# Seven block products for eight in four of the twelve value chunks of a two-layer encoder's first layer

## The chip, the cores and the metric

The kernel runs on one core of a Trainium2 chip. The metric is the time of one execution on the device in microseconds, median of three runs: 1988.34 us before (1987.91 to 1989.26). PE is the matrix engine, DVE the vector engine, ACT the scalar engine, POOL and SP two further engines that here mostly issue transfers.

## The reference, cut to what matters

The model is an encoder of two layers over 256 tokens of width 2048 in fp32; layer 0 mixes tokens by attention over a neighbourhood, layer 1 by grouped-query attention, and both attend to 256 memory tokens. The change touches the projection of layer 0 that makes the values `v`, 12 heads of 128:

```
def reference(x, mem, mem_norm, attn_norm, mlp_norm, a_w_in, ...):
    m = rms_norm(mem, mem_norm)
    h = x
    for i in range(DEPTH):
        n = rms_norm(h, attn_norm[i])
        if i % N_MIXERS == 0:
            z = n @ a_w_in[j]
            q, k, v, qm = jnp.split(z, [MIX_WIDTH, 2 * MIX_WIDTH, 3 * MIX_WIDTH], axis=-1)
            mix = neighbourhood_attention(split_heads(q, N_MIX_HEADS), split_heads(k, N_MIX_HEADS),
                                          split_heads(v, N_MIX_HEADS), a_rpb[j])
...
        h = h + jnp.concatenate([mix, cross], axis=-1) @ w_o[i]
        n = rms_norm(h, mlp_norm[i])
        h = h + jnp.square(jax.nn.relu(n @ w_up[i])) @ w_down[i]
    return rms_norm(h, final_norm)
```

## The kernel before

**Arithmetic.** Every fp32 operand is split into a high and a low part (`split`, L519 on ACT writes the high part, L520 on DVE the low part), and each product of two operands is three matmuls: high by high, high by low, low by high.

**Chunks and halves.** A weight chunk is 1 MB (`raw`, 128 partitions by 2048 values, a ring of three, loaded by SP). It is used in two halves of 1024 columns of storage; each half is split into one place of a ring of four `hi` and one of four `lo`. Projections of two kinds use them. "S" products (L422, `ps_s`) keep an activation's or weight's 128x128 block still and move 128x256: 24 matmuls a half. "M" products (L399, L402, L403, `ps_m`) move 128x512: 12 matmuls a half.

**Layer 0's input projection.** After the memory's keys and values and the four memory heads' queries come three groups. A group is a value projection for four heads (chunks `w_av[g*4]` to `w_av[g*4+3]`, eight halves, summed in two banks of PSUM) and then, for each of its four heads, a query chunk and a key chunk (S). When a head's key is done its attention follows: scores `sc_ps` on PE, softmax on DVE and ACT (`sc`, `nm`, `rs`), DVE's transposition `sc_t`, transfers into `pT_t` by SP, the split of `pT_t`, and `av` on PE, whose split lands in `cat`. The attention of a group's last head falls into the value projection of the next group.

**What sets the order.** `plan` lists the pieces of work and `run_all` (L456) walks through their halves in `order`. Ahead of the half that PE is to run, it issues the stages of later halves: the load 8 ahead, a `lift` 8 ahead, `pre` 5 and the split (`prep`) 3 ahead. `later(n, ...)` puts a function n halves on. A scheduler with a model of the times then sets the order of instructions on each engine; on the chip each engine runs its list in that order.

**Seven for eight, where the kernel has it already.** Layer 0's output projection uses a scheme with seven block products for eight in two chunks (`crossed_works`, L1065; PSUM `ps_x`, and `s_x`, `t_x` for sums of weight blocks). The activations' sums for it are made by `sums_ahead` (L1046): ACT copies 128x512 of `cat` into `c_x` (L1056), a transfer issued by POOL adds 256 KB to it on the way (L1057), DVE makes three sums (L1061 to L1063), and a split puts them into `a_x`. A `lift` of the same kind stands in the up-projection (L1353, L1354, `t<-b`): an ACT copy, and a transfer of 256 KB that adds.

Of the kernel before, what the change touches and what calls it, by code (L numbers as in the profile page):

```python
# [24 lines left out]
NH = 12  # L25
# [8 lines left out]
CH = 2048  # L34
HALF = CH // 2
# [11 lines left out]

CROSSED = (3, 0)
CROSSED_NB = 2
CROSSED_AT = 64  # L50

MOVING_AT = 160

# [10 lines left out]
LONGER = {"hi": 128, "lo": 128}  # L64
# [93 lines left out]
class Grain:  # L158


    def __init__(self, run, after=None, load=None, pre=None, prep=None, ahead=(8, 5, 3), lift=None):
        self.run, self.after, self.stages = run, after, (load, lift, pre, prep)
        self.ahead = ahead[0], 8, *ahead[1:]
        self.kind, self.last_block = "M", False


@with_exitstack
def encoder_kernel(ctx: ExitStack, tc: tile.TileContext, t: dict, out: bass.AP):
    nc = tc.nc
# [55 lines left out]
    for q in range(4):  # L225
        s = slice(q * 512, (q + 1) * 512)
# [151 lines left out]
    def later(n, fn, *args):  # L378
        pending.append((state["tick"] + n, fn, args))
# [48 lines left out]
    def begin():  # L428

        box["memT"] = at.cat.tile([P, KT, 512], F32R, tag="cat", name="memT")  # L430
        tiles = {}
        for w in plan[:FIRST_CHUNKS]:
            w.start(w)
        for q in range(4):
            s = slice(q % 2 * 512, q % 2 * 512 + 512)

            def memory(k):
                return split_pair(box["memT"], mem0[:, k * SEQ : (k + 1) * SEQ], G_MEM, k)

            def weights(c):  # L440
                if q % 2 == 0:
                    tiles[c] = new_half("S")
                return split(*(x[:, s] for x in tiles[c]), raws[c][:, q * 512 : (q + 1) * 512])


            for fn, n in ((memory, 4 * q), (memory, 4 * q + 1), (weights, 0), (memory, 4 * q + 2), (memory, 4 * q + 3),
                          (weights, 1), (weights, 2)):
                for ins in fn(n):
                    if q == 0:
                        pin(ins)  # L450
            for c, w in enumerate(plan[:FIRST_CHUNKS]):
# [65 lines left out]
    def split(dst_hi, dst_lo, src):  # L517

        first = nc.scalar.activation(dst_hi, src, AF.Copy)  # L519
        return first, nc.vector.tensor_tensor(dst_lo, src, dst_hi.bitcast(F32), op=ALU.subtract)  # L520
# [40 lines left out]
    def summed(ps, name, row, factor=1.0):  # L561

        s = at.work.tile([P, SEQ], F32, tag="sum_s", name=f"{name}_s")
        nc.vector.scalar_tensor_tensor(s, ps, factor, row, op0=ALU.mult, op1=ALU.mult)
        return s
# [203 lines left out]
    def values(tag, name, bufs=None):  # L769
        return at.work.tile([P, 2, NT, 512], F32R, tag=tag, bufs=bufs, name=name)  # L770

    def head_of(v, hd):
        return lambda part, kt: v[:, part, kt, hd * HD : (hd + 1) * HD]

    def put_value(dst, ps, r):
        nc.scalar.activation(dst[:, 0], ps, AF.Copy, scale=r)
        nc.vector.scalar_tensor_tensor(dst[:, 1], ps, r, dst[:, 0].bitcast(F32), op0=ALU.mult, op1=ALU.subtract)

    def put_values(v, ps, scale):
        for i in range(NT):  # L780
            put_value(v[:, :, i, :], ps[i], scale[:, i : i + 1])
# [103 lines left out]
    add_mem(1)  # L885


    GH = 4

    def a_v_done(g):  # L890
        def f(w):
            box["v", g] = values("l4", "va")
            put_values(box["v", g], w.ps, box["x_col"])
        return f

    def a_q_done(hd):
        def f(w):
# [6 lines left out]
    def a_k_done(hd):  # L904
        def f(w):
# [10 lines left out]
    def a_qm_done(hd):  # L916
        def f(w):
            if hd == 0:
                box["cat"] = at.cat.tile([P, KT, 512], F32R, tag="cat", name="cat0")
            q = at.work.tile([P, 512], F32R, tag="b_y", name="qmT")  # L920
            s = summed(w.ps, "qm", box["x_row"], SCALE)
            split(q[:, :SEQ], q[:, SEQ:], s)
            attention([(q, box["km"][:, hd, :], None, head_of(box["vm"], hd), NH + hd, box["cat"])], 1)
        return f

    for hd in range(NMH):
        add_s(t["w_aqm"][hd], get("nT"), a_qm_done(hd))
    for g in range(NH // GH):
        add_m([t["w_av"][g * 4 + c] for c in range(4)], parts_of("nT"), a_v_done(g))
        for hd in range(g * GH, (g + 1) * GH):  # L930
            add_s(t["w_aq"][hd], get("nT"), a_q_done(hd))
            add_s(t["w_ak"][hd], get("nT"), a_k_done(hd))
# [138 lines left out]
    def crossed_works(done):  # L1071
# [28 lines left out]
        def half(n, c, hf):  # L1100
# [29 lines left out]
            def run():  # L1130
# [52 lines left out]

    FIRST = ("p3", 6, 0), ("p1", 0, 1), ("p2", 2, 2)
    SECOND = ("p7", 4, 0), ("p6", 5, 1), ("p4", 1, 2), ("p5", 3, 3)

    def half_of_side(raw, hf, place=0):  # L1190
        s = slice(place // 4, place // 4 + HALF)
# [139 lines left out]
    def down_grains(layer, n, begins, ends, sooner):  # L1331
# [80 lines left out]

    def open_strassen(layer):
# [421 lines left out]
    def blocks(nb):  # L1835
        return [t["w_b"][nb * 4 + c] for c in range(4)]
# [186 lines left out]
```

## Time and profile before

| what | us |
|---|---|
| median of three runs | 1988.34 |
| the profiled execution, whole | 1987.95 |
| its span, first to last instruction | 1986.1 |
| two heads' query and key chunks ahead of the middle value group | 166.07 to 189.79 |
| middle value group | 189.79 to 212.86 |
| two heads ahead of the third value group | 235.70 to 259.43 |
| third value group | 259.43 to 282.50 |
| four heads behind it, with the `c_x` sums | 282.50 to 329.80 |

Times inside the span count from its first instruction. The 1.85 us between span and whole execution lie around the span. A row of the timeline gives the start, the duration and, in brackets, how long the engine had been idle and what released it. A group of PE rows has the modelled end of each matmul, so that the pitch from start to start says more than the duration.

### The profile page before, as it was taken

Reading aid. Unit: us, or ns where it says so; the run is one execution under the profiler, and the core shown is the slowest. Engines: PE = TensorE matmul, PEld = TensorE weight load, DVE = VectorE, ACT = ScalarE, POOL = GpSimd, SP = SyncE. Lnnn points to the kernel's source line nnn. Section 1 sums busy time; section 2 is a strip of 40 time slices with the busy share of each in tenths; the row PEclk is TensorE's granted clock in tenths of the full one; section 3 lists DMA queues with packets and bytes.
Section 4 is the critical chain, followed back from the end, with each engine's and each line's share of the span. In section 5 each row is a group of like instructions: output and inputs, shape, how many; then the busy total and the mean of one; then the engine's idle time right before and its main releaser. Section 6 shows DMA issues by size and latency. Waiting matters only on the chain.

```text
span 1986.1 us, 33222 instructions
## 1 busy us (share of the span) xinstructions
PE 1976.1 (99%) x12852; PEld 1797.4 (90%) x12852; DVE 1743.9 (88%) x2132; ACT 1450.1 (73%) x2123; POOL 156.5 (8%) x209
## 2 busy tenths in 40 slices
PE   9999999999999999999999999999999999999998
PEld 8999999899999999999998888889999999999997
DVE  7777768799999999999999869789999999999997
ACT  6655556677887778777887656668788777877786
POOL 0000000000000000000001001001000000000001
PEclk9999999999999999999999999999999999999999
DMA  8856666777777777777778765668777777777775
GB/s 296 319 195 203 207 195 195 275 223 240 228 227 236 232 226 235 232 242 227 223 227 230 266 213 176 220 207 256 238 229 227 237 224 232 236 234 240 225 225 158
DMA packets 113951, 454.57 MB, mean 229 GB/s; under 512 B 19073, under 2 KB 43777, under 8 KB 66433
## 3 DMA queue, kind: packets, MB, share of 16 engines
q1 hardware_dynamic: 92320, 414.43, 60.9%
q0 software_dynamic: 21184, 37.50, 10.7%
q8 instruction: 101, 1.65, 0.3%
q10 hardware_dynamic: 288, 0.52, 0.1%
q14 instruction: 58, 0.47, 0.1%
HBM read 397.78 MB, written 4.19 MB: 202 GB/s over the span
## 4 chain that ended last, share of the span: by engine, by line
PE 97%; DVE 1%; DMA 1%; issue 1%; ACT 0%; SPq 0%; POOL 0%; DVEq 0%; POOLq 0%; ACTq 0%
PE ps_u L422 35%; PE p L1386 10%; PE p L1389 10%; PE p L1390 10%; PE ps_s L422 9%; PE ps_m L402 7%; PE ps_m L403 7%; PE ps_m L399 7%; DMA c_x<-cat 0%; PE sc_ps L617 0%; PE sc_ps L616 0%; PE sc_ps L615 0%; PE av L711 0%; PE av L712 0%; PE av L713 0%
## 5 line engine op out<-in xcount | busy, mean ns | idle before, releaser
L422 PE MATMUL ps_u<-hT,uh 128*128 128x256 f32 x3812 | 662.9, 276 | 0.0
L422 PEld LDWEIGHTS ps_u<-hT,uh 128*128 128x128 f32 x3812 | 578.7, 188 | 4.8
L422 PE MATMUL ps_u<-hT,ul 128*128 128x256 f32 x1964 | 542.7, 276 | 0.0
L519 ACT ACTIVATE uh<-raw_U 128x1024 fp32r<-128x1024 f32 x258 | 273.4, 1061 | 157.2 <-PE ps_u L422 155.2
L422 PEld LDWEIGHTS ps_u<-hT,ul 128*128 128x128 f32 x1964 | 368.8, 188 | 0.0
L519 ACT ACTIVATE hi<-raw 128x1024 fp32r<-128x1024 f32 (+2 forms) x215 | 221.0, 1032 | 160.8 <-PE ps_m L403 81.0
L520 DVE TENSOR_TENSOR lo<-raw,hi 128x1024 fp32r<-128x1024 f32 (+2 forms) x215 | 253.3, 1184 | 85.4 <-ACT hi L519 84.6
L520 DVE TENSOR_TENSOR ul<-raw_U,uh 128x1024 fp32r<-128x1024 f32 x258 | 313.9, 1218 | 11.6 <-ACT uh L519 11.6
L520 DVE TENSOR_TENSOR tl<-t,th 128x2048 fp32r<-128x2048 f32 x120 | 274.8, 2290 | 51.7 <-ACT th L519 51.2
L519 ACT ACTIVATE th<-t 128x2048 fp32r<-128x2048 f32 x120 | 230.6, 1922 | 92.6 <-PE p L1390 92.6
L520 DVE TENSOR_TENSOR bl<-b,bh 128x1536 fp32r<-128x1536 f32 x120 | 210.1, 1751 | 0.3 <-ACT bh L519 0.3
L1354 POOL DMA_DIRECT2D t<-b x120 | 103.4, 862 | 1175.6 <-ACT t L1353 1073.8
L1386 PE MATMUL p<-th,a_s 128*128 128x512 f32 x480 | 187.4, 391 | 0.0
L1389 PE MATMUL p<-tl,a_s 128*128 128x512 f32 x480 | 187.2, 390 | 0.0
L1390 PE MATMUL p<-th,a_s 128*128 128x512 f32 x480 | 186.7, 389 | 0.0
L519 ACT ACTIVATE bh<-b 128x1536 fp32r<-128x1536 f32 x120 | 178.8, 1490 | 3.4
L422 PE MATMUL ps_s<-nT,hi 128*128 128x256 f32 x896 | 154.6, 277 | 0.0
L1389 PE MATMUL p<-bl,a_s 128*128 128x512 f32 x360 | 140.1, 389 | 0.0
L1386 PE MATMUL p<-bh,a_s 128*128 128x512 f32 x360 | 140.1, 389 | 0.0
L1390 PE MATMUL p<-bh,a_s 128*128 128x512 f32 x360 | 140.0, 389 | 0.0
L422 PEld LDWEIGHTS ps_s<-nT,hi 128*128 128x128 f32 x896 | 135.3, 188 | 0.2
L422 PE MATMUL ps_s<-nT,lo 128*128 128x256 f32 x448 | 124.2, 277 | 0.0
(343 smaller groups left out, 3713.2 us busy)
## 6 DMA issues: line engine op xcount, KB each, us to landing
raw_U<-in_w_up SPq DMA_DIRECT2D x128, 1024.0 KB, 6.3
b<-in_w_pair SPq DMA_DIRECT2D x120, 1024.0 KB, 5.8
raw<-in_w_o SPq DMA_DIRECT2D x32, 1024.0 KB, 5.0
t<-b POOLq DMA_DIRECT2D x120, 256.0 KB, 6.6
raw<-in_w_b SPq DMA_DIRECT2D x21, 1024.0 KB, 5.8
raw<-in_w_av SPq DMA_DIRECT2D x12, 1024.0 KB, 5.0
raw<-in_w_aq SPq DMA_DIRECT2D x12, 1024.0 KB, 4.9
raw<-in_w_ak SPq DMA_DIRECT2D x12, 1024.0 KB, 4.9
```

What stands on the lines that cost most here:

```text
L399: first = nc.tensor.matmul(ps, ah, hi[:, s], start=st, stop=False)
L402: nc.tensor.matmul(ps, ah, lo[:, s], start=False, stop=False)
L403: final = nc.tensor.matmul(ps, al, hi[:, s], start=False, stop=sp)
L422: ins = nc.tensor.matmul(ps, x, acts[:, k, part], start=k == n == 0, stop=k == KT - 1 and n == 2)
L519: first = nc.scalar.activation(dst_hi, src, AF.Copy)
L520: return first, nc.vector.tensor_tensor(dst_lo, src, dst_hi.bitcast(F32), op=ALU.subtract)
L1354: nc.gpsimd.dma_start(s[:, 3, :], b[:, 1, :], accum_op=ALU.add)
L1386: ins = nc.tensor.matmul(ps, a[:, 0, ai, :], hi[:, s], start=entered, stop=False, skip_group_check=True)
L1389: nc.tensor.matmul(ps, a[:, 0, ai, :], lo[:, s], start=False, stop=False, skip_group_check=True)
L1390: nc.tensor.matmul(ps, a[:, 1, ai, :], hi[:, s], start=False, stop=ends, skip_group_check=True)
```

## The change

Chunk 0 of every group, and chunk 1 of the middle group too, are computed by seven block products for eight: four of twelve chunks, eight of 24 halves. For a half, the left side is 2 x 2 blocks (two blocks of 128 rows of tokens by two blocks of 128 of the width) and the right side 2 x 2 blocks of 128x256. Seven products in three matmuls each are 21 matmuls of 128x256, in place of 12 of 128x512.

- **`combined`** makes the left sides' sums once: for each of the four pairs an ACT copy (128x512), a transfer of POOL that adds (256 KB), three DVE sums and a split. They lie in places of `cat` that heads 4 to 11 fill later. It runs from the start of the memory heads' queries on (`COMBINED_AT`).
- **The right side's sums**, per half: `lift` (an ACT copy of 512 into `s_v`, and a transfer of POOL that adds 256 KB), `pre` (two DVE sums of 128x256), `prep` (a split of 768 of the raw blocks and one of 1024 of the sums, two places of the ring and not one). `s_v` has two places, so the third crossed half's lift in a group waits until the first one's sums are split, and the fourth's until the second's.
- **`fold`** after the last crossed half of a group: two ACT copies of 512 out of `ps_x`, four DVE subtractions of 256. **`done`**: two DVE sums of 512 of `ps_m` and these, and then `put_value` from SBUF and not from PSUM.
- A value group holds four banks of PSUM and not two.
- `VALUES_ORDER` sets halves in turn: plain, crossed, plain, crossed and four plain in the first and third group (crossed halves are 6 and 7); plain, crossed, plain, crossed, plain, crossed, crossed, plain in the middle one.
- The host permutes the blocks in the crossed chunks of `w_av`. `CROSSED_AT` shifts where the output projection's crossed splits lie in the ring's place.

```
+VALUES_CROSSED = (0,), (0, 1), (0,)
+VALUES_ORDER = {1: (0, 6, 1, 7, 2, 3, 4, 5), 2: (0, 4, 1, 5, 2, 6, 7, 3)}
+COMBINED_AT = (1, 2, 6, 8)
...
+            if w.mixed:
+                order[-8:] = [order[n - 8] for n in w.mixed]
...
+    FIRST = ("p3", 6, 0), ("p1", 0, 1), ("p2", 2, 2)
+    SECOND = ("p7", 4, 0), ("p6", 5, 1), ("p4", 1, 2), ("p5", 3, 3)
...
+        def together(n):
+            k, c = pairs[n], room[:, n % 2, :4].rearrange("p (k b) j -> p k (b j)", k=2)
+            both = box["nT"][:, k : k + 2, :].bitcast(F32)
+            nc.scalar.activation(c, both[:, :, :SEQ], AF.Copy)
+            nc.gpsimd.dma_start(c, both[:, :, SEQ:], accum_op=ALU.add)
...
+        for n, at_tick in zip(range(len(pairs)), COMBINED_AT):
+            later(at_tick, together, n)
+            later(at_tick + 2, summed, n)
...
+        def fold():
+            z = room(0)
+            for n in range(NT):
+                nc.scalar.activation(z[:, 2 - 2 * n : 4 - 2 * n].rearrange("p a b -> p (a b)"), sums["two"][n], AF.Copy)
+            for d, x, y in ((3, 3, 2), (0, 3, 0), (3, 3, 1), (1, 1, 0)):
+                nc.vector.tensor_tensor(z[:, d], z[:, x], z[:, y], op=ALU.subtract)
...
+            def lift():
+                own["s"] = room(hf)
+                s, b = own["s"][:, 0:4:3], blocks()
+                nc.scalar.activation(s, b[:, 3, None, :].to_broadcast([P, 2, SEQ]), AF.Copy)
+                nc.gpsimd.dma_start(s, b[:, 0:2], accum_op=ALU.add)
+
+            def pre():
+                s, b = own["s"], blocks()
+                for d in (1, 2):
+                    nc.vector.tensor_tensor(s[:, d], s[:, d - 1], b[:, d], op=ALU.add)
+
+            def prep():
+                own["b"], own["t"] = ([at.ring.tile([P, HALF + x], F32R, tag=y, bufs=4, name=y)[:, VALUES_AT // 4 :][:, : m * SEQ]
+                                       for y, x in LONGER.items()] for m in (3, 4))
+                split(*own["b"], blocks()[:, :3].rearrange("p a b -> p (a b)"))
+                box["weights"] = split(*own["t"], own["s"].rearrange("p a b -> p (a b)"))
...
+                for products, (bh, bl) in ((FIRST, own["b"]), (SECOND, own["t"])):
+                    for name, ai, bi in products:
+                        ah, al = acts[ai]
+                        s = slice(bi * SEQ, (bi + 1) * SEQ)
...
+                            own[name] = nc.tensor.matmul(ps, ah, bh[:, s], start=st, stop=False, skip_group_check=True)
+                        nc.tensor.matmul(ps, ah, bl[:, s], start=False, stop=False, skip_group_check=True)
+                        nc.tensor.matmul(ps, al, bh[:, s], start=False, stop=sp, skip_group_check=True)
+
+            g_ = Grain(run, fold if last else None, load if hf == 0 else None, pre, prep, lift=lift)
+            g_.ahead = 7, 5, 4, 3
+            return g_
...
-        add_m([t["w_av"][g * 4 + c] for c in range(4)], parts_of("nT"), a_v_done(g))
+        crossed_values(g)
```

The order of instructions shows the change at three places. Numbers behind a name are those of the tile.

First place: DVE's list before the change, two heads ahead of the middle value group, from the split of one head's `pT_t` to the next head's query.

```order
L520 TENSOR_TENSOR lo_2036<-raw_2033,hi_2035 128x1024
L520 TENSOR_TENSOR pT_t_1820<-pT_t_1820 128x320
L599 TENSOR_TENSOR sc_1945<-sc_ps_1940,bias_1928 128x320
L601 TENSOR_TENSOR sc_1945<-sc_ps_1940,sc_1945 128x320
L573 TENSOR_REDUCE nm_1948<-sc_1945 128x2
L520 TENSOR_TENSOR lo_2067<-raw_2033,hi_2066 128x1024
L578 RECIPROCAL rs_1953<-sm_1949 128x2
L564 SCALAR_TENSOR_TENSOR q_s_2029<-ps_s_1963,x_row_970 128x256
```

The same stretch of DVE's list in the changed kernel (L528 is the `split` line there, L989 the sums of `pre`, `raw_2140` the first crossed chunk of the middle group).

```order
L528 TENSOR_TENSOR lo_2110<-raw_2107,hi_2109 128x1024
L528 TENSOR_TENSOR pT_t_1894<-pT_t_1894 128x320
L989 TENSOR_TENSOR s_v_2247<-s_v_2247,raw_2140 128x256
L607 TENSOR_TENSOR sc_2019<-sc_ps_2014,bias_2002 128x320
L989 TENSOR_TENSOR s_v_2247<-s_v_2247,raw_2140 128x256
L609 TENSOR_TENSOR sc_2019<-sc_ps_2014,sc_2019 128x320
L528 TENSOR_TENSOR lo_2143<-raw_2107,hi_2142 128x1024
L581 TENSOR_REDUCE nm_2022<-sc_2019 128x2
L572 SCALAR_TENSOR_TENSOR q_s_2103<-ps_s_2037,x_row_970 128x256
L989 TENSOR_TENSOR s_v_2247<-s_v_2247,raw_2140 128x256
L726 TENSOR_TENSOR av_s_2009<-av_2004,av_s_2009 128x256
L989 TENSOR_TENSOR s_v_2247<-s_v_2247,raw_2140 128x256
```

The first sum of `pre`, which needs the transfer into `s_v`, now stands ahead of the softmax, and three more are between its rows. From there to this block's `kT` (`kT_2094` before, `kT_2170` now) there are four sums and one `lo` more. On PE that head's scores begin 28 matmuls of the last key and one `av` (four matmuls) ahead of the first value product; before, 52 and one `av`.

Second place: DVE's list before the change inside the middle value group, around the softmax of the preceding group's last head.

```order
L520 TENSOR_TENSOR kT_2265<-k_s_2266,kT_2265 128x256
L520 TENSOR_TENSOR lo_2350<-raw_2347,hi_2349 128x1024
L520 TENSOR_TENSOR pT_t_2162<-pT_t_2162 128x320
L520 TENSOR_TENSOR lo_2368<-raw_2347,hi_2367 128x1024
L599 TENSOR_TENSOR sc_2287<-sc_ps_2282,bias_2270 128x320
L601 TENSOR_TENSOR sc_2287<-sc_ps_2282,sc_2287 128x320
L573 TENSOR_REDUCE nm_2290<-sc_2287 128x2
L520 TENSOR_TENSOR lo_2396<-raw_2393,hi_2395 128x1024
L578 RECIPROCAL rs_2295<-sm_2291 128x2
```

The same stretch now, behind `kT` and the first sum for the third crossed half (`raw_2318` is the second crossed chunk, `lo_2425` and `lo_2427` belong to the second crossed half, `lo_2460` to the third plain one).

```order
L528 TENSOR_TENSOR lo_2425<-raw_2140,hi_2424 128x768
L989 TENSOR_TENSOR s_v_2247<-s_v_2247,raw_2318 128x256
L528 TENSOR_TENSOR lo_2427<-s_v_2247,hi_2426 128x1024
L528 TENSOR_TENSOR pT_t_2238<-pT_t_2238 128x320
L607 TENSOR_TENSOR sc_2376<-sc_ps_2371,bias_2359 128x320
L609 TENSOR_TENSOR sc_2376<-sc_ps_2371,sc_2376 128x320
L581 TENSOR_REDUCE nm_2379<-sc_2376 128x2
L586 RECIPROCAL rs_2384<-sm_2380 128x2
L588 TENSOR_SCALAR sc_2376<-sc_2376,rs_2384 128x160 x2
L666 STREAM_TRANSPOSE sc_t_2410<-sc_2376 128x2x4x32
L668 STREAM_TRANSPOSE sc_t_2410<-sc_2376 128x64
L528 TENSOR_TENSOR lo_2460<-raw_2457,hi_2459 128x1024
```

No `lo` stands between `nm` and `rs` any more, and the third plain half's `lo` comes behind the whole softmax.

Third place: PE's list of the changed kernel at the third plain half of the middle group (L405, L408 and L409 are the three plain matmuls, L1011 to L1013 the three of a crossed product).

```order
L1011 MATMUL ps_x_2395<-hi_2426,cat0_1153 128x256
L1012 MATMUL ps_x_2395<-lo_2427,cat0_1153 128x256
L1013 MATMUL ps_x_2395<-hi_2426,cat0_1153 128x256
L405 MATMUL ps_m_2396<-hi_2459,nT0_919 128x512
L405 MATMUL ps_m_2397<-hi_2459,nT0_919 128x512
L1011 MATMUL ps_x_2394<-hi_2479,nT0_919 128x256
L408 MATMUL ps_m_2396<-lo_2460,nT0_919 128x512
L409 MATMUL ps_m_2396<-hi_2459,nT0_919 128x512
```

Before the change the three matmuls of a product stand together at every half, as at this one.

```order
L402 MATMUL ps_m_2305<-lo_2332,nT0_919 128x512
L403 MATMUL ps_m_2305<-hi_2331,nT0_919 128x512
L399 MATMUL ps_m_2306<-hi_2331,nT0_919 128x512
L402 MATMUL ps_m_2306<-lo_2332,nT0_919 128x512
L403 MATMUL ps_m_2306<-hi_2331,nT0_919 128x512
```

Three products with `hi` alone, one of them of the next half, have been set ahead of the first that needs the new `lo_2460`.

More of the change, by code (lines that the diff above doesn't have):

```diff
@@ L49 @@
 CROSSED_NB = 2
-CROSSED_AT = 64
+CROSSED_AT = 192
+VALUES_CROSSED = (0,), (0, 1), (0,)
+VALUES_ORDER = {1: (0, 6, 1, 7, 2, 3, 4, 5), 2: (0, 4, 1, 5, 2, 6, 7, 3)}
+VALUES_AT = 192
+COMBINED_AT = (1, 2, 6, 8)
 MOVING_AT = 160
@@ L91, in __init__ @@
         self.early = self.behind = self.last_block = self.held = False
+        self.mixed = None
 class Shifted:
@@ L163, in __init__ @@
         self.ahead = ahead[0], 8, *ahead[1:]
-        self.kind, self.last_block = "M", False
+        self.kind, self.last_block, self.mixed = "M", False, None
 @with_exitstack
@@ L885, in encoder_kernel, with combined, summed @@
     add_mem(1)
+    FIRST = ("p3", 6, 0), ("p1", 0, 1), ("p2", 2, 2)
+    SECOND = ("p7", 4, 0), ("p6", 5, 1), ("p4", 1, 2), ("p5", 3, 3)
     GH = 4
[L890 to L894, printed above, removed]
+    def combined(chunks):
+        pairs = [4 * c + 2 * hf for c in chunks for hf in range(2)]
+        room = at.work.tile([P, 2, 8, P], F32, tag="l4", name="c_v")
+        for n, c in enumerate(chunks):
+            heads = NH - 4 - 4 * n
+            both = box["cat"][:, heads : heads + 4, :].rearrange("p (n b) (m j) -> p n b m j", n=2, j=P)
+            for hf in range(2):
+                box["combined", c, hf] = both[:, hf]
+        def together(n):
[3 more added lines that the diff above has]
+            nc.gpsimd.dma_start(c, both[:, :, SEQ:], accum_op=ALU.add)
+        def summed(n):
+            c, a = room[:, n % 2], box["combined", pairs[n] // 4, n % 2]
+            nc.vector.tensor_tensor(c[:, 4, :], c[:, 0, :], c[:, 2, :], op=ALU.subtract)
+            nc.vector.tensor_tensor(c[:, 5:7, :], c[:, 0:8:4, :], c[:, None, 1, :].to_broadcast([P, 2, P]), op=ALU.add)
+            nc.vector.tensor_tensor(c[:, 7, :], c[:, 3, :], c[:, 6, :], op=ALU.subtract)
+            split(a[:, 0], a[:, 1], c[:, 4:])
+        for n, at_tick in zip(range(len(pairs)), COMBINED_AT):
+            later(at_tick, together, n)
+            later(at_tick + 2, summed, n)
@@ new lines, in crossed_values, with begin, room, done @@
+    def crossed_values(g):
+        crossed = VALUES_CROSSED[g]
+        plain = [c for c in range(4) if c not in crossed]
+        sums = {}
+        halves = [(c, hf) for c in crossed for hf in range(2)]
+        def begin(w):
+            if "direct" not in sums:
+                two, direct = ([at.acc.tile([P, 512], F32, tag="acc", name=n) for _ in range(NT)] for n in ("ps_x", "ps_m"))
+                sums.update(direct=direct, two=two, p4=direct[0][:, :SEQ], p2=direct[1][:, :SEQ], p3=direct[1][:, SEQ:],
+                            p1=two[0][:, :SEQ], p6=two[0][:, SEQ:], p7=two[1][:, :SEQ], p5=two[1][:, SEQ:])
+            w.ps = sums["direct"]
+        def room(hf):
+            if "room" not in sums:
+                sums["room"] = at.work.tile([P, 2, 4, SEQ], F32, tag="l4", name="s_v")
+            return sums["room"][:, hf]
+        def fold():
[4 more added lines that the diff above has]
+                nc.vector.tensor_tensor(z[:, d], z[:, x], z[:, y], op=ALU.subtract)
+        def done(w):
+            z, v = room(0), values("l4", "va")
+            box["v", g] = v
+            for i in range(NT):
+                own = z[:, 2 * i : 2 * i + 2].rearrange("p a b -> p (a b)")
+                nc.vector.tensor_tensor(own, sums["direct"][i], own, op=ALU.add)
+            for i in range(NT):
+                own = z[:, 2 * i : 2 * i + 2].rearrange("p a b -> p (a b)")
+                put_value(v[:, :, i, :], own, box["x_col"][:, i : i + 1])
+        for n, c in enumerate(plain):
+            plan.append(Work("M", t["w_av"][g * 4 + c], parts_of("nT"), c * 4, n == 0, n == len(plain) - 1, begin, done))
+        raws = {}
+        def half(n, c, hf):
+            own = {}
+            first, last = n == 0, n == len(halves) - 1
+            def load():
+                raws[c] = at.ring.tile([P, CH], F32, tag="raw", bufs=3, name="raw")
+                box["load"] = nc.sync.dma_start(raws[c], t["w_av"][g * 4 + c])
+            def blocks():
+                return raws[c].rearrange("p (x a b) -> p x a b", x=2, a=4)[:, hf]
+            def lift():
[12 more added lines that the diff above has]
+                box["weights"] = split(*own["t"], own["s"].rearrange("p a b -> p (a b)"))
+            def run():
+                k = 4 * c + 2 * hf
+                made = [tuple(box["combined", c, hf][:, part, m] for part in range(2)) for m in range(4)]
+                acts = parts_of("nT")
+                acts = [acts(k, 1), acts(k + 1, 0), acts(k + 1, 1)] + made
+                for products, (bh, bl) in ((FIRST, own["b"]), (SECOND, own["t"])):
+                    for name, ai, bi in products:
+                        ah, al = acts[ai]
+                        s = slice(bi * SEQ, (bi + 1) * SEQ)
+                        st = first and name in ("p1", "p7")
+                        sp = last and name in ("p1", "p7", "p6", "p5")
+                        ps = sums[name]
+                        after = {"p6": "p1", "p5": "p7"}.get(name) if first else None
+                        with tc.issue_after(own[after].ins) if after else nullcontext():
+                            own[name] = nc.tensor.matmul(ps, ah, bh[:, s], start=st, stop=False, skip_group_check=True)
[4 more added lines that the diff above has]
+            return g_
+        plan.extend(half(n, c, hf) for n, (c, hf) in enumerate(halves))
+        plan[-1].mixed = VALUES_ORDER[len(crossed)]
@@ L919, in f @@
                 box["cat"] = at.cat.tile([P, KT, 512], F32R, tag="cat", name="cat0")
+                combined(VALUES_CROSSED[1])
             q = at.work.tile([P, 512], F32R, tag="b_y", name="qmT")
@@ L1178, in add_o @@
                 plan[-1].behind = plan[-2].behind = plan[-1].last_block = True
-    FIRST = ("p3", 6, 0), ("p1", 0, 1), ("p2", 2, 2)
-    SECOND = ("p7", 4, 0), ("p6", 5, 1), ("p4", 1, 2), ("p5", 3, 3)
     def half_of_side(raw, hf, place=0):
@@ L2009 @@
         arrays["w_o0"][CROSSED_NB * 4 + c] = x.reshape(P, 2, 4, 2 * P)[:, :, [3, 0, 2, 1]].reshape(P, CH)
+    for g, chunks in enumerate(VALUES_CROSSED):
+        for c in chunks:
+            x = arrays["w_av"][g * 4 + c]
+            arrays["w_av"][g * 4 + c] = x.reshape(P, 2, 4, 2 * P)[:, :, [3, 0, 2, 1]].reshape(P, CH)
     arrays["w_first"] = np.concatenate([by_blocks(x) for x in arrays["w_km0"][:FIRST_CHUNKS]])
```

## Prediction

> **What bounds the kernel now.** I read the page's busy times first, then the chain that ended last, then the stages by windows, and in them the timeline of PE, DVE, POOL and SP.
>
> ```profile
> span 1986.1 us, 33222 instructions
> PE 1976.1 (99%) x12852; PEld 1797.4 (90%) x12852; DVE 1743.9 (88%) x2132; ACT 1450.1 (73%) x2123; POOL 156.5 (8%) x209
> PE 97%; DVE 1%; DMA 1%; issue 1%; ACT 0%; SPq 0%; POOL 0%; DVEq 0%; POOLq 0%; ACTq 0%
> ```
>
> PE is busy for 99% of the span and holds 97% of the chain, so only fewer or faster matmuls can make the kernel faster, and anything else can only make PE wait. The stages that the change touches:
>
> ```profile
> core 0: us, PE busy (x) PEld busy (x) DVE busy (x) ACT busy (x) POOL busy (x), PEclk, DMA share, GB/s
> 166.07:189.79 23.72, 23.72 (x208) 23.72 (x208) 19.74 (x38) 14.00 (x26) 0.37 (x4) 1.00 0.64 212
> 189.79:212.86 23.07, 23.07 (x108) 19.22 (x107) 15.15 (x25) 11.76 (x18) 0.18 (x2) 1.00 0.58 193
> 282.50:329.80 47.30, 46.87 (x410) 46.70 (x409) 37.08 (x70) 27.35 (x48) 5.39 (x10) 1.00 0.72 214
> ```
>
> In the value group (second row) PE never waits, DVE is idle for 23.07 - 15.15 = 7.9 us and ACT for 11.3. In the heads ahead of it (first row) DVE has only 4.0 us left in 23.72. The third row holds the one wait of PE here: 47.30 - 46.87 = 0.43 us, where the `c_x` sums fall.
>
> **What the change removes.** The pitch of the matmuls, from PE's timeline:
>
> ```profile
> 189.00 0.28 PE L422 MATMUL ps_s<-nT,lo 128*128 128x256 f32 x1
> 189.34 0.28 PE L422 MATMUL ps_s<-nT,lo 128*128 128x256 f32 x1
> 189.68 0.28 PE L422 MATMUL ps_s<-nT,lo 128*128 128x256 f32 x1
> 189.79 0.40 PE L399 MATMUL ps_m<-hi,nT 128*128 128x512 f32 x1
> 195.26 0.39 PE L399 MATMUL ps_m<-hi,nT 128*128 128x512 f32 x1
> ```
>
> Six matmuls of 128x256 take 0.68 us (one `lo` in three), 113.8 ns each as in longer stretches: 192 of them and the 16 of the attention fill the 23.72 us of the window above. From 189.79 to 195.26 lie 24 of 128x512: 5.47 us, 227.7 ns each. A plain half is 12 x 227.7 = 2.73 us, a crossed one 21 x 113.8 = 2.39. Eight halves: 8 x 0.34 = **-2.7 us**, 0.14% of the time. This is all that can be won. A measurement of this kernel tells about 0.2% from no change, 4.0 us, so no version of the gain alone counts as faster.
>
> [...] By the rows above the ratio here is 113.8 to 227.7, a half, so the sum keeps the full gain.
>
> **What it adds on DVE and ACT.** Prices from the scheme's existing instructions and the splits:
>
> ```profile
> L1056 ACT ACTIVATE c_x<-cat x4: 613/631/635, 284.3 to 297.5; 128x512 f32<-128x512 f32 x4
> L520 DVE TENSOR_TENSOR a_x<-c_x,a_x x4: 682/684/685, 332.5 to 339.3; 128x512 fp32r<-128x512 f32 x4
> ...
> L1092 ACT ACTIVATE z_x<-ps_x x2: 577/578/580, 396.8 to 397.3; 128x512 f32<-128x512 f32 x2
> ...
> L520 DVE TENSOR_TENSOR lo<-raw,hi 128x1024 fp32r<-128x1024 f32 (+2 forms) x215 | 253.3, 1184 | 85.4 <-ACT hi L519 84.6
> ...
> 295.03 0.75 DVE L1062 TENSOR_TENSOR c_x<-c_x 128x256 f32<-128x256 f32 x2
> ```
>
> Two sums of 128x256 follow each other in 0.75 us, 0.34 to 0.42 each. A crossed half replaces one `lo` of 1024 (1.14 from start to start) by one of 768 (between 0.68 for 512 and 1.18 for 1024, say 0.87), one of 1024, and two sums (0.7): 1.6 us more. The middle group has four, 6.3, then the fold (4 x 0.34) and two sums of 512 (1.3): 9 us more on DVE, against 7.9 idle, in a group 1.4 us shorter. Part of it lies in the heads ahead or behind. So DVE, hidden until now, is about full there. The first and third group get 5.8 us each and keep some 1.5. ACT gets per half a copy of 0.63 and 0.75 more of split, 5.5 us in the middle group with two copies of 0.58: 11.3 idle cover it. The four left-side sums lie beside the memory heads, where I cost them with the first group, below.
>
> **The waits: how late the lifts land.** DVE works its list in order, so a sum that waits for POOL's transfer holds the softmax behind it. Before has the same thing with `c_x`:
>
> ```profile
> 285.28 2.48 POOL L1057 DMA_DIRECT2D c_x<-cat  x2 [1.13 <-ACT c_x L1056]
> ...
> 285.47 0.33 SPq L282 DMA_DIRECT2D raw<-in_w_aq  x1
> ...
> 293.12 0.29 DVE L1061 TENSOR_TENSOR c_x<-c_x 128x128 f32<-128x128 f32 x1 [1.99 <-DMA c_x<-cat]
> 294.82 0.29 DVE L1061 TENSOR_TENSOR c_x<-c_x 128x128 f32<-128x128 f32 x1 [1.41 <-DMA c_x<-cat]
> ...
> DMA to landing us min/median/max: 4.0/8.3/9.8
> ...
> t<-b POOLq DMA_DIRECT2D x120, 256.0 KB, 6.6
> ...
> 1400.00:1500.00 100.00, 100.00 (x672) 91.71 (x671) 93.27 (x98) 80.73 (x105) 8.61 (x10) 1.00 0.75 231
> ```
>
> Issued beside a raw load, two transfers landed after 7.8 and 8.8 us; over four they were 4.0 to 9.8. The 120 of `t<-b`, equal in size, had a median of 6.6 where transfers fill 0.75 of the queues' time. The groups here stand at 0.58 to 0.64, and one lift goes at a time: I take a landing time L of **6.0 us**, nearest to `t<-b`, and keep 4.0 and 8.3 as ends.
>
> [...]
>
> *Ahead of the middle and the third group.* The places on DVE, and SP's load beside which the lift goes:
>
> ```profile
> 168.76 0.53 SPq L282 DMA_DIRECT2D raw<-in_w_av  x1
> ...
> 170.98 0.48 DVE L520 TENSOR_TENSOR pT_t<-pT_t 128x320 fp32r<-128x320 f32 x1
> 171.56 0.49 DVE L599 TENSOR_TENSOR sc<-sc_ps,bias 128x320 f32<-128x320 f32 x1
> ...
> 179.08 1.23 DVE L520 TENSOR_TENSOR lo<-raw,hi 128x1024 fp32r<-128x1024 f32 x1 [0.62 <-ACT hi L519]
> 180.22 0.42 DVE L520 TENSOR_TENSOR kT<-k_s,kT 128x256 fp32r<-128x256 f32 x1
> ```
>
> The first `s_v` sum stands behind `pT_t`, so DVE reaches it at 171.4. The lift goes some tenths ahead of the load at 168.76, as `c_x` did (285.28 against 285.47): about 168.1, landing at 168.1 + L. From 171.56 to 180.64, the end of `kT`, are 9.08 us, 0.62 of them idle; with four sums (4 x 0.34) and one more `lo` (1.14) 10.9. So `kT` ends at 179.0 + L. The scores need it where 28 matmuls, an `av` and they themselves (3.19 + 0.48 + 0.48) still come before 189.79: at 185.6. They are late from L = 6.6, and by 1.2 at 7.8; the `av` behind them, with another `lo` and a query ahead of it on DVE, adds 0.7. I let the wait grow by 1 us per us of L from 5.9: at 6.0 **0.1 each, 0.2 for both**; at 4.0 nothing; at 8.3 2.4 each.
>
> *Inside the middle group*, in us from its start. DVE comes 1.5 late (`kT` above, then rows of 6.4 to the last `k_s`, in before at 190.00, 0.2). `lo`, `cat` and `kT` (1.9) bring it to 3.6 and to the third crossed half's first sum. That lift had to wait for the first one's `lo` and lands at about L - 0.3, 5.7. Then sums and splits of 2.7, `pT_t` 0.5, three softmax rows 1.5, ACT's exponentials 1.1, normalizing and transposing 1.4, and `lo` of the third plain half 1.1: ready at 14.0. PE is there after two plain halves (5.47), two crossed (4.78), scores and `av` (about 1.0), so at 11.25, and three products that need no `lo` carry it to 11.8. It waits **2.3**. Before, this cannot happen:
>
> ```profile
> 196.61 1.23 DVE L520 TENSOR_TENSOR lo<-raw,hi 128x1024 fp32r<-128x1024 f32 x1 [1.10 <-ACT hi L519]
> 199.87 1.23 DVE L520 TENSOR_TENSOR lo<-raw,hi 128x1024 fp32r<-128x1024 f32 x1 [0.58 <-ACT hi L519]
> ```
>
> DVE there waits for ACT's `hi` at each half, so it is ahead. The wait follows L from 3.7: 0.3 at 4.0, 4.6 at 8.3. What comes later in the group (the fourth lift, `t`, the last `lo`) is ready by my count within 0.3 us of PE's need once that wait has been paid, so I add nothing.
>
> *First group and the left-side sums.* The nearest row is what the `c_x` sums cost, 0.43 us; bounds 0 to 1.5. I take **0.5**. The fold and the final sums lie in front of `va`, which no `av` needs for some 10 us, since a query, a key and a softmax come first: nothing.
>
> **Sum.** -2.7 + 0.2 + 2.3 + 0.5 = **+0.3 us**. On the profiled execution (1987.95, of which 1986.1 span and 1.85 around it) that is 1988.2; on the median of 1988.34, 0.4 higher, 1988.6. I give 1988.4.
>
> **Rivals.**
>
> *The gain stays.* L is 4.0, or DVE's slack absorbs more than I count: -2.7 + 0.3 + 0.5 = -1.9, 1986.0; with no wait at all 1985.2. For it: lone transfers of 4.0, and the `c_x` waits, 3.4 us of idle DVE, cost PE 0.43 only. Against: PE's list already takes three products out of turn at the third plain half.
>
> *DVE's queue stands behind late lifts* (the other side). At L = 8.3, the median of `c_x`: two waits of 2.4, one of 4.6, and 0.5: -2.7 + 9.9 = +7.2, 1995.1. For it: the lifts go beside a raw load as those did, and DVE has 4.0 us of slack in the heads ahead. Against: lower share of the queues, and no pair of lifts together. It decides slower from the L where 2 x (L - 5.9) + (L - 3.7) + 0.5 - 2.7 = 4.0: L = 7.2.
>
> *Narrow products cost more than half.* Were the pitch in proportion to the rows' durations, 0.28 against 0.39, a crossed half would be 21 x 0.72 x 227.7 = 3.4 us, +0.7 for each of eight: +5.7 with no wait, about 1993.7. Against: the pitch measured above, in the same kind of split operands. [...]
>
> *The change doesn't do what it says*, for instance the crossed halves end up as long as plain ones through waits for weights of their own: then about 1988 to 1991.
>
> **Chances.** Forecast 0.40, gain stays 0.32, late lifts 0.24, narrow products 0.02, not as described 0.02. Faster by over 0.2% needs more than the whole gain, and I leave 0.02 of the second case for it; slower by over 0.2% is late lifts and narrow products, 0.26; the rest, 0.72, is within. The range goes from the full gain, 1985.3, to L = 8.3 on the profiled run, 1995.0.
>
> **What would show it.** Right: crossed products at a pitch of 113.8 ns, and in the middle group's window PE's busy time 1.4 us less. Each lift's time to landing, in the row of `s_v` transfers, decides between the first three cases: near 4, 6 or 8. On DVE `s_v` sums idle "<-DMA s_v"; on PE one wait of about 2 us at the third plain half of the middle group, "<-DVE lo", and almost none at the scores ahead of it. Wrong: waits on PE in the third group's or the first group's crossed halves, on ACT, or on PSUM's banks, or a changed raw load.

## The result and the profile after

The changed kernel takes **2008.53 us** (2005.1 to 2009.19, four runs) against 1988.42 before: a ratio of 1.0097, interval 1.008 to 1.0115. It is slower by 20 us, where the forecast was no change, 1988.4 with a range up to 1995.0. The sign was that of the rival "late lifts", the size nearly three times its 7.2 us. Of all runs below one was slow, 2468.66 us of e7, at a mean granted clock of 0.752 and not 0.998 or 0.999.

The page of the profiled execution (2008.85 us), its busy times and the chain that ended last:

```profile
span 2006.9 us, 33493 instructions
PE 1984.0 (99%) x12924; PEld 1807.2 (90%) x12924; DVE 1766.9 (88%) x2190; ACT 1466.5 (73%) x2153; POOL 171.3 (9%) x221
...
PE 90%; DMA 4%; DVE 3%; issue 2%; ACT 1%; SPq 0%; POOL 0%; POOLq 0%; DVEq 0%; ACTq 0%
```

PE's share still reads 99%, and this is misleading twice. PE's busy time has grown by 7.9 us though there is less to multiply, and its share of the chain has fallen from 97% to 90%, with transfers and DVE in its place. The view of the waits of PE, summed by the line that waited and the one waited for (us in total, times, longest):

```profile
PE sc_ps L602 <- DVE kT L528: 6.5, 3, 3.5
PE sc_ps L623 <- ACT qmT L527: 2.3, 1, 2.3
PE ps_m L405 <- ACT hi L527: 2.3, 1, 2.3
PE av L719 <- ACT pT_t L527: 1.9, 1, 1.9
PE idle L254 <- POOL mhalf L248: 1.0, 1, 1.0
PE ps_s L428 <- ACT hi L527: 0.6, 1, 0.6
```

The last two rows belong to the start. The others are six waits of 13.0 us: at the first memory head (2.3), at the last memory head's `av` (1.9), at the scores ahead of the middle group (1.3), at its third plain half (2.3), at the scores ahead of the third group (1.7) and behind it, beside the `c_x` sums (3.5). Before there was one of 0.43.

The rest of the loss is the clock. Windows of 3.41 us around four of the waits (span of the window, PE busy, and, behind the busy times, the granted clock):

```profile
104.58:107.99 3.41, 1.49 (x13) 1.28 (x11) 1.18 (x5) 2.18 (x4) 2.11 (x2) 1.00 1.06 381
107.99:111.41 3.42, 3.03 (x14) 3.03 (x15) 3.30 (x7) 1.95 (x4) 0.29 (x1) 0.50 1.07 312
148.96:152.37 3.41, 1.52 (x14) 1.32 (x13) 1.51 (x3) 0.82 (x2) 0.00 (x0) 1.00 1.01 380
152.37:155.78 3.41, 3.41 (x17) 3.41 (x18) 3.41 (x5) 3.05 (x4) 0.00 (x0) 0.50 0.32 89
...
268.42:271.83 3.41, 1.74 (x15) 1.62 (x14) 2.54 (x4) 1.43 (x4) 0.00 (x0) 1.00 0.32 55
271.83:275.25 3.42, 3.42 (x28) 3.27 (x27) 3.05 (x6) 2.36 (x7) 0.18 (x2) 1.00 0.84 314
312.79:316.20 3.41, 0.87 (x8) 0.67 (x6) 3.06 (x7) 2.44 (x5) 1.19 (x1) 1.00 0.00 0
316.20:319.61 3.41, 2.44 (x11) 2.45 (x12) 2.82 (x5) 1.40 (x3) 1.19 (x1) 0.50 0.97 178
319.61:323.03 3.42, 3.42 (x18) 3.42 (x18) 3.31 (x9) 1.92 (x6) 0.00 (x0) 0.50 1.03 272
```

After a window in which PE was busy for 1.49, 1.52 or 0.87 us, the next ran at half the clock (0.50); after one with 1.74 it stayed full (1.00). In the four slow windows PE worked for 3.03 + 3.41 + 2.44 + 3.42 = 12.3 us at half speed, and lost 6.1.

One more part is no part of the change. The same matmul of the memory's value projection starts later before any new instruction has run (PE's timeline of the kernel before, then of the changed one):

```profile
77.43 0.61 PE L399 MATMUL ps_m<-hi,memT 128*128 128x512 f32 x2
```

```profile
79.21 0.61 PE L405 MATMUL ps_m<-hi,memT 128*128 128x512 f32 x2
```

This execution started 1.8 us behind. That is scatter of the start: the twelve profiles come to the first matmul of this projection between 71.9 and 73.7 us, the kernel before at 72.0, e1 below, with the same code up to there, at 71.9, and this execution, at 73.7, as the last. So the 20.8 us of span are 12.6 of waits, 6.1 of slow clock and 1.8 of the start, less some 2.0 of matmuls that were saved (below). That gives 18.5; some 1 us, by estimate, goes into the six restarts, since a matmul lasts 0.28 us and is followed after 0.11 only in a row, and about 1.3 stay unassigned.

**What PE waited for.** DVE's, POOL's and SP's timelines ahead of the middle group, where the prediction had worked the lift out:

```profile
178.13 0.53 SPq L288 DMA_DIRECT2D raw<-in_w_ak  x1
...
178.43 2.40 POOL L984 DMA_DIRECT2D s_v<-raw  x2 [21.90 <-ACT s_v L983]
...
180.71 0.48 DVE L528 TENSOR_TENSOR pT_t<-pT_t 128x320 fp32r<-128x320 f32 x1
185.71 0.42 DVE L989 TENSOR_TENSOR s_v<-s_v,raw 128x256 f32<-128x256 f32 x1 [4.52 <-DMA s_v<-raw]
...
195.83 0.41 DVE L528 TENSOR_TENSOR kT<-k_s,kT 128x256 fp32r<-128x256 f32 x1
...
259.57 0.43 DVE L989 TENSOR_TENSOR s_v<-s_v,raw 128x256 f32<-128x256 f32 x1 [4.92 <-DMA s_v<-raw]
...
313.14 0.29 DVE L1188 TENSOR_TENSOR c_x<-c_x 128x128 f32<-128x128 f32 x1 [3.89 <-DMA c_x<-cat]
```

Both lifts of this chunk go together, beside a raw load, and the first lands after 7.3 us. DVE stands at the sum from 181.2 to 185.7, with the softmax behind it, and `kT` comes at 195.8 + 0.4, while PE has been waiting since 195.1. The same happens ahead of the third group (4.92) and with `c_x` (3.89). The landings of the eight lifts, from the view of the tile `s_v`, and of the four left-side transfers, from that of `c_v`:

```profile
DMA to landing us min/median/max: 3.9/7.7/8.7
```

```profile
DMA to landing us min/median/max: 3.8/9.7/13.1
```

In the view of the waits of DVE the three kinds stand with 25.2 us together:

```profile
DVE s_v L989 <- DMA s_v<-raw: 11.4, 5, 4.9
...
DVE c_v L919 <- DMA c_v<-nT: 8.3, 3, 4.1
DVE c_x L1188 <- DMA c_x<-cat: 5.5, 2, 3.9
```

### The profile page after: what moved, and what is told of

It reads as the page before. It is cut to its first block, busy times and chain, and to the rows that moved or that the text cites. A ratio compares the mean times of both kernels' runs of the same rounds, so it can differ in the third digit from the quotient of the medians.

```text
span 2006.9 us, 33493 instructions
## 1 busy us (share of the span) xinstructions
PE 1984.0 (99%) x12924; PEld 1807.2 (90%) x12924; DVE 1766.9 (88%) x2190; ACT 1466.5 (73%) x2153; POOL 171.3 (9%) x221
## 4 chain that ended last, share of the span: by engine, by line
PE 90%; DMA 4%; DVE 3%; issue 2%; ACT 1%; SPq 0%; POOL 0%; POOLq 0%; DVEq 0%; ACTq 0%
PE ps_u L428 35%; PE p L1510 10%; PE p L1513 10%; PE p L1514 9%; PE ps_m L408 6%; PE ps_m L409 6%; PE ps_m L405 6%; PE ps_s L428 6%; DMA raw<-in_w_av 1%; DMA s_v<-raw 1%; DVE lo L528 1%; DMA c_v<-nT 0%; DMA c_x<-cat 0%; DMA pT_t<-sc_t 0%; PE sc_ps L623 0%
## 5 line engine op out<-in xcount | busy, mean ns | idle before, releaser
L528 DVE TENSOR_TENSOR ul<-raw_U,uh 128x1024 fp32r<-128x1024 f32 x258 | 313.8, 1218 | 11.5 <-ACT uh L527 11.5
L528 DVE TENSOR_TENSOR tl<-t,th 128x2048 fp32r<-128x2048 f32 x120 | 274.8, 2290 | 51.7 <-ACT th L527 51.2
L528 DVE TENSOR_TENSOR lo<-raw,hi 128x1024 fp32r<-128x1024 f32 (+2 forms) x215 | 250.8, 1174 | 62.2 <-ACT hi L527 61.3
L528 DVE TENSOR_TENSOR bl<-b,bh 128x1536 fp32r<-128x1536 f32 x120 | 210.2, 1751 | 0.6 <-ACT bh L527 0.6
L428 PE MATMUL ps_s<-nT,hi 128*128 128x256 f32 x896 | 159.7, 282 | 0.0
L428 PEld LDWEIGHTS ps_s<-nT,hi 128*128 128x128 f32 x896 | 139.4, 193 | 0.2
```

Source lines behind the costliest of these rows:

```text
L428: ins = nc.tensor.matmul(ps, x, acts[:, k, part], start=k == n == 0, stop=k == KT - 1 and n == 2)
```

## The experiments

Four theories. **A**: DVE's list has sums standing where the transfers haven't landed, and the softmax behind them makes PE wait. **B**: DVE is full, whatever it waits for. **C**: chunks used in turn hold the three places of the raw ring longer, and raw loads come late. **E**: the transfers themselves slow down others.

**The lifts on DVE** (e1): one DVE sum of 512 in place of ACT copy and transfer.

```
-                nc.scalar.activation(s, b[:, 3, None, :].to_broadcast([P, 2, SEQ]), AF.Copy)
-                nc.gpsimd.dma_start(s, b[:, 0:2], accum_op=ALU.add)
+                nc.vector.tensor_tensor(s[:, 0:4:3], b[:, 3, None, :].to_broadcast([P, 2, SEQ]), b[:, 0:2], op=ALU.add)
```

> The eight lifts (ACT copy and POOL transfer into s_v) become one DVE sum of 128x512 each; the left-side sums keep their transfers. Theory A (late transfers hold DVE's list and with it the softmax): the waits of PE ahead of the middle and third groups (1.3 and 1.7 us) go, the one at the third plain half (2.3) shrinks below 1, those at the memory heads (2.3) and behind the third group (3.5) stay with their slow-clock stretches: about 2001 to 2004. Theory B (DVE is simply full): 8 x 0.68 = 5.5 us more on DVE, all waits stay or grow: 2008 or more. Theory C (raw loads come late because chunks are used in turn and hold the ring of three): the 2.3 at the third plain half stays, 2004 to 2007.

1994.56 us (1992.48 to 1999.09), ratio 1.0031 [1.002, 1.0042]: 14 us less than the changed kernel, more than A forecast. The waits ahead of the groups are gone, the one at the middle group's third plain half is 0.8. Those at the memory heads, which A expected to stay, are down to 0.5; those beside `c_x` stay (4.4) with one slow window (mean granted clock 0.998, in the changed kernel 0.995). B is out: DVE has more to do, and PE waits less.

**The left-side sums on DVE** (e2):

```
-            nc.scalar.activation(c, both[:, :, :SEQ], AF.Copy)
-            nc.gpsimd.dma_start(c, both[:, :, SEQ:], accum_op=ALU.add)
+            nc.vector.tensor_tensor(c, both[:, :, :SEQ], both[:, :, SEQ:], op=ALU.add)
```

> Only the four left-side sums lose their ACT copy and POOL transfer and become DVE sums of 128x512; the lifts keep theirs. A: the wait at the first memory head (2.3 us) and the slow-clock stretch behind it (1.7) go, perhaps the av wait at 150 (1.9 + 1.7) too, as DVE is no longer late there: 2001 to 2005. B: nothing is won, 2008 or more. C: no change, about 2008.

2003.38 us (1998.6 to 2005.33), 1.0065 [1.0048, 1.0082]. The waits at 106.1 and 150.4 are gone, but the first group's lifts take their place: DVE waits 1.7 and 4.4 us for them ahead of a memory head's query, and PE 3.9 for that; and the value projection of the memory waits 1.7 for a `lo` at 78, behind the new DVE sums. Three slow windows are left (mean granted clock 0.996). A in kind; the two transfers cover for each other, so undoing one is worth less than its own wait.

**All on DVE** (e3): e1, e2 and the same edit for the older `c_x`.

> All such transfers of the attention stage gone: lifts, left-side sums and the older c_x sums of the output projection as DVE sums of 128x512. A: all waits on DVE below 0.5 us, no slow-clock stretch, the 2.7 us of fewer matmuls come through: 1985 to 1989. B: DVE has 16 x 0.68 = 11 us more: 2008 or more. C: some 2 to 5 us of waits remain at the halves that follow a late raw load: 1989 to 1993.

1988.92 us (1987.93 to 1990.58), 1.0001 [0.9992, 1.001]. The waits of PE in it:

```profile
PE ps_m L408 <- DVE lo L528: 1.7, 1, 1.7
PE idle L254 <- POOL mhalf L248: 1.0, 1, 1.0
PE ps_m L405 <- ACT hi L527: 0.8, 1, 0.8
PE ps_s L428 <- DVE lo L528: 0.2, 1, 0.2
```

The whole loss of 20 us hangs on these sixteen transfers, and every slow window went with them: the mean granted clock is 0.999 as in the kernel before. What stands against the saved matmuls is the wait at 78 and 0.8 at the third plain half. The raw load of that half was issued by SP at 197.6, behind six transfers into `pT_t`, and landed at 202.6; its `hi` begins at 202.7, and the trace names an `av` of PE as what ended last before it. So C is worth 0.8 us at most, and even that is not shown.

**No taking of turns** (e4): a chunk's halves one behind the other.

```
-VALUES_ORDER = {1: (0, 6, 1, 7, 2, 3, 4, 5), 2: (0, 4, 1, 5, 2, 6, 7, 3)}
+VALUES_ORDER = {1: (0, 1, 2, 3, 6, 7, 4, 5), 2: (0, 1, 4, 5, 6, 7, 2, 3)}
```

> The changed kernel with all its transfers, but a chunk's two halves always one behind the other (first and third group: two plain, two plain, the crossed pair, two plain; middle: two plain, four crossed, two plain). C: the raw ring is freed chunk by chunk, the 2.3 us at the third plain half go, but waits for lifts stay: about 2004. A: the lifts are reached later (their halves come later), so waits move, but as many: 2002 to 2012; crossed halves back to back need the third lift after the first half's split, so a new wait of 3 to 6 us on ps_x in the middle group.

2013.58 us (2012.65 to 2014.46), 1.0124 [1.0109, 1.0139]. In this order the middle group's third and fourth lift go into the places of the first and second before these are split, so two of its halves use other sums (POOL issues these lifts at 194.2, and the first split of `s_v` there begins at 207.1), and the expected wait for the split cannot show. PE waits 2.2 at the memory heads, 3.2 at the first one's `av`, 2.3 at the scores ahead of the middle group, 3.2 at an `av` later and five times less than 2: as many as before, moved. Halves in turn are not the cause.

**Lifts earlier** (e8), transfers kept:

```
-            g_.ahead = 7, 5, 4, 3
+            g_.ahead = 8, 7, 4, 3
```

> The changed kernel with its transfers, loads 8 and lifts 7 halves ahead in place of 7 and 5. A: a lift that goes some 5 us earlier has landed when DVE comes to its sum; waits ahead of middle and third group go, those of the memory heads and c_x stay: 1998 to 2004. C: the raw ring has no free place earlier, so the lift goes at the same time: 2006 to 2010.

2006.04 us (2004.47 to 2008.93), 1.0089 [1.0075, 1.0103]. Here too the middle group's third and fourth lift overwrite the sums of the first two (issued at 194.2, the first split at 203.5). The time is what C forecast, but not for C's reason. The lift does go earlier, and DVE's sum with it (POOL's and DVE's timelines):

```profile
172.76 2.41 POOL L984 DMA_DIRECT2D s_v<-raw  x2 [15.28 <-ACT s_v L983]
...
175.21 1.19 DVE L528 TENSOR_TENSOR lo<-raw,hi 128x1024 fp32r<-128x1024 f32 x1
180.61 0.43 DVE L989 TENSOR_TENSOR s_v<-s_v,raw 128x256 f32<-128x256 f32 x1 [4.22 <-DMA s_v<-raw]
```

PE waits longer than in the changed kernel, 15 us in all against 13, 7.2 of them at a memory head, where DVE stands 6.9 us for the first group's lift. The scheduler has moved the sum along, from behind `pT_t` to ahead of the `k_s` and `kT` that stood before it. DVE comes to it 3.6 us after the issue, as it came 2.8 us after it in the changed kernel; the transfer takes 7.9. It looks as though the model that sets the lists takes these transfers to land in some 3 us; the model itself was not looked into.

**The sums held back** (e11), transfers of lifts and left sides kept, `c_x` on DVE:

```
-            g_.ahead = 7, 5, 4, 3
+            g_.ahead = 7, 5, 3, 3
...
-                for d in (1, 2):
-                    nc.vector.tensor_tensor(s[:, d], s[:, d - 1], b[:, d], op=ALU.add)
+                with tc.issue_after(box["weights"][1].ins):
+                    for d in (1, 2):
+                        nc.vector.tensor_tensor(s[:, d], s[:, d - 1], b[:, d], op=ALU.add)
...
-            later(at_tick + 2, summed, n)
+            later(at_tick + 4, lambda n=n: past(lambda: summed(n), box["weights"]))
```

> The lifts and the left-side sums keep their ACT copies and POOL transfers as in the changed kernel; only DVE's sums behind them are held back in its list (the lift's sums a half later and behind the split of the half before, the left-side sums two halves later and behind that split); the c_x sums are on DVE as in e3. A, that it is DVE waiting in its order for transfers which its list takes to be there: most waits go with the transfers still running, 1986 to 1992. Rival E, that the transfers themselves slow raw loads and the other queues: the waits stay in the third plain half and at the heads, 1996 or more.

1990.83 us (1990.12 to 1992.44), 1.0011 [1.0002, 1.0021]. The waits of PE, and the landings of the lifts:

```profile
PE ps_x L1012 <- ACT hi L527: 1.2, 2, 0.8
PE idle L254 <- POOL mhalf L248: 1.0, 1, 1.0
PE av L719 <- ACT pT_t L527: 0.5, 1, 0.5
PE ps_m L405 <- ACT hi L527: 0.3, 1, 0.3
```

```profile
DMA to landing us min/median/max: 3.8/7.6/11.3
```

This settles it for the lifts and the left sides. The lifts land as late as before, a median of 7.6 us against 7.7, the latest after 11.3 against 8.7, the left sides go by transfer too, and the waits of PE are 2.0 us with no slow window (mean granted clock 0.999). Of the 13 us before, the 3.5 beside `c_x` left with those transfers, so 9.5 is what the 2.0 compares with. E is out; what cost the time is where the sums stand in DVE's list. The run is still 2.1 us above the kernel before it, about its 2.0 of waits.

**What remains, and the better kernels.** e6 is e3 with the left-side sums behind the split of their time, e7 the same with one crossed chunk in the middle group too, e12 with the two crossed chunks in the first group and one in each of the others; e10 is the kernel before with `c_x` on DVE alone.

```
+            with tc.issue_after(box["weights"][1].ins):
+                nc.vector.tensor_tensor(c, both[:, :, :SEQ], both[:, :, SEQ:], op=ALU.add)
...
-VALUES_CROSSED = (0,), (0, 1), (0,)
+VALUES_CROSSED = (0,), (0,), (0,)
```

> As e3 (all sums on DVE), and the left-side sums are kept behind the weights' split of their time, so that they no longer stand among the memory's value projection. If the wait of 1.7 us at 78 in e3 came from these sums ahead of a lo: it goes, 1986.5 to 1988. If it came from something else there: 1988.9 as e3. The wait of about 1 us at the middle group's third plain half stays under both.

> As e6, but one crossed chunk in the middle group too (six halves in place of eight: 6 x 0.34 = 2.0 us less work for PE than before). If the middle group's wait comes from its fuller DVE or from its chunks in turn with late raw loads: it goes, 1986.2 to 1987.5. If a single crossed chunk makes it too: 1987.3 to 1989.

> The kernel before with only the four c_x sums of the output projection on DVE in place of ACT copy and transfer. A: its one wait of 0.43 us goes: 0.2 to 0.6 us faster, 1987.9 to 1988.7 beside 1988.4 to 1988.9, which five rounds hardly tell. B: as slow or slower.

> As e6, with the two crossed chunks in the first group and one in each of the others (eight halves, 2.7 us less work). If only the middle group's fuller DVE stood against its second chunk: 1985.6 to 1986.5, a little below e7. If two chunks in a group make a wait in any group: 1986.5 to 1989.

| kernel | us | ratio to before | waits of PE behind the start, in the profile, us |
|---|---|---|---|
| e6 | 1986.72 (1985.79 to 1988.43) | 0.999 [0.9981, 0.9999] | 1.1, 0.5 |
| e7 | 1986.24 (1985.44 to 2468.66) | 0.9988 [0.9979, 0.9997] | none behind the start |
| e10 | 1987.66 (1987.38 to 1988.41) | 0.9995 [0.9987, 1.0004] | none behind the start |
| e12 | 1989.28 (1988.3 to 1991.5) | 1.0005 [0.9996, 1.0014] | 2.4 in three, 0.8, 0.8 |

e7 beats both kernels: 2.5 us under the 1988.73 of before in the same rounds, by the median of eleven runs. Six halves at the 0.25 us worked out below make 1.5 of it and the old `c_x` wait 0.4; the rest stays unassigned. From e6 it cannot be told apart by these times. Its busy times, and all its waits of PE:

```profile
PE 1974.5 (100%) x12906; PEld 1799.2 (91%) x12906; DVE 1767.3 (89%) x2188; ACT 1456.7 (73%) x2133; POOL 153.1 (8%) x205
...
PE idle L254 <- POOL mhalf L248: 1.0, 1, 1.0
```

In e6 the wait at 78 is down to 0.5, so the left-side sums had made most of it. The one at the third plain half, which was expected to stay, is gone, and a new one of 1.1 stands at an `av` behind the middle group; e7, with one crossed chunk there, has neither. In e12 (its profile is that of the slowest of its eleven runs, 1991.5) the two waits of 0.8 lie in the first group, which has two crossed chunks, but the three at an `av`, 0.6 to 0.9, lie ahead of, or behind, groups with one. So the runs show that these kernels wait where e7 does not, and not that the second chunk as such makes every wait. Nor do they bear out theory B: ahead of the 1.1 in e6 and the three in e12, DVE stood idle for 2.9 to 3.2 us, until a `pT_t` had come by SP's transfers and been split on ACT. Why these came late was not tried. e10's gain is within its interval, and cannot be told apart from the start's scatter; the one wait of before is gone.

## Why the prediction was wrong

*The gain* was mis-sized. The pitch was taken from S products, 113.8 ns. Crossed products go slower (PE's timeline of the changed kernel):

```profile
205.22 0.28 PE L1011 MATMUL ps_x<-hi,cat 128*128 128x256 f32 x1
...
205.93 0.28 PE L1013 MATMUL ps_x<-hi,cat 128*128 128x256 f32 x1
```

Six steps in 0.71 us: 118 ns, the same as the older `ps_x` products have. A half is 21 x 0.118 = 2.48 us, so it saves 0.25 and not 0.34, and eight save 2.0 and not 2.7.

*L = 6.0* failed: the lifts had a median of 7.7 us. The reason given, that one lift goes at a time, was wrong for six of the eight: POOL issues two together, as it did with `c_x`, and the nearer row was theirs, 8.3. Yet it does not take a pair to make a lift slow: the last lift of the middle group went alone, beside raw loads, and took 8.0; the one before it, alone with no raw load under way, 3.9. Nor was L the main failure: put into the prediction's own formulas, 7.7 gives 2 x 1.8 + 4.0 + 0.5 - 2.7 = +5.4 us, a quarter of the loss.

*Ahead of the middle and third group* the mechanism was right and its size too, given L. At 7.7 the formula gives 1.8 each; DVE waited 4.52 and 4.92 us, and PE 1.3 and 1.7.

*Inside the middle group* 2.3 us were forecast at the third plain half and 2.3 came, but through ACT's `hi`, not DVE's `lo`: the half's raw load was issued at 208.3, behind SP's transfers into `pT_t` and as DVE's late sum let go of its place in the ring, and landed at 213.3. The agreement is partly chance.

*First group and left-side sums, 0.5* is the step that failed most. The `c_v` transfers were set down as lying beside the memory heads, though the same section had priced `c_x` by the waits they make. Two of them were issued still earlier, at 80 us, in the memory's value projection. They took up to 13.1 us to land, DVE stood 8.3 us in three waits for them, and with the first group's lifts behind them PE waited 2.3 and 1.9, each with a slow window after it: some 7.4 us in place of 0.5 (e1 and e2, which remove one of the two each, leave waits of 0.5 and 3.9). At the second wait itself it is a transfer into `pT_t` that comes late; that DVE's standing put it there is inferred from e1 and e2, each of which removes it. The price of one earlier wait, 0.43, was taken where slack had been there to absorb 3.4 us of DVE's; here, to judge by the waits, it was not.

*Left out altogether:* that the old `c_x` sums would come to stand nearer to their transfers, and the clock. The second `c_x` sum could begin 9.0 us after POOL's first issue, much as before (9.5), but DVE came to it 5.1 us after that issue and not 8.1; PE's wait grew from 0.43 to 3.5, with two slow windows behind it. A wait was priced by its own length, but three of six were followed by 3.4 or 6.8 us at half speed: 6 us, more than twice the gain.

*The rivals.* Narrow products at more than half their price: 118 against 114, a tenth of what the rival asked. "The gain stays" is what e7 shows, where PE waits for nothing behind the start.

## What to carry to other kernels

An engine that works a list in order must not have a transfer's consumer near the transfer's issue (here DVE came to a sum 2.8 us after the issue of a transfer that took 7.3, and stood for 4.5 with the softmax behind it): look in the list how much work stands between them, and compare it with the landing time of the nearest such transfer under the same load, not with the time that the scheduler supposes; issuing earlier does not help where the scheduler moves the consumer along (e8, 2006.04 us). On a kernel whose matrix engine is full, a sum of 0.7 us on an engine with slack was cheaper here than a transfer that takes none of its time and landed after 7.7 in the median (1988.92 us against 2008.53). Price a wait of the matrix engine with what the clock does after it, here 3.4 or 6.8 us at half speed after three of six.

## What the runs showed of the hardware

In the changed kernel the granted clock fell from 1.00 to 0.50 at 108.0, 152.4 and 316.2 us and rose again at 111.4, 155.8 and 323.1: all of them whole steps of 3.41 us apart, 63 steps from the first to the last. A wait well under such a window was enough: those at the memory heads were 2.3 and 1.9 us. In e2, too, a window with PE busy for 1.69 of 3.41 us was followed by one at half the clock (same columns as above):

```profile
208.60:212.01 3.41, 1.69 (x14) 1.49 (x13) 2.31 (x8) 2.19 (x6) 1.16 (x3) 1.00 1.02 358
212.01:215.42 3.41, 3.41 (x8) 2.38 (x9) 3.41 (x5) 2.48 (x4) 0.00 (x0) 0.50 1.01 237
```

With 1.74 busy (the row at 268.42) it stayed full, and the wait of 2.3 us at 212 in the changed kernel fell across two windows with 2.07 and 2.35 us busy, and cost no clock. The dividing line in these rows lies between 1.69 and 1.74 us of 3.41, about one half; whether it is the share of time or a count of work was not tried. On the same grid in the changed kernel, from 73 to 357 us, the three windows at full clock with 1.52 or less were each followed by one at half, and every one with 1.74 or more by a full one. At half clock the line lay higher: after a slow window with 2.44 us busy (the row at 316.20) the next was slow too, after those with 3.03 and 3.42 (107.99 and 319.61) it was full. So the wait of 3.5 us, which fell into two windows with 0.87 and 2.44 us busy, cost two slow ones.

Transfers of 256 KB that add, issued by POOL, most of them in pairs and beside raw loads of 1 MB, landed after a median of 7.7 us (eight lifts) and 9.7 (four `c_v`), the least 3.8. The one lift that had no raw load beside it, issued at 202.75 between a load that landed at 201.7 and one issued at 208.3, landed after 3.9.
